# An encoder block on one core: sixteen gate projections as eight pairs of seven half-size products

## The chip, the cores and the metric

The kernel runs on one core of a Trainium2 chip. The metric is the device time of one execution in microseconds (us), the median of several runs. Five engines work side by side, each through its own instructions in order: TensorE (PE in the profile, with its weight loads as PEld), VectorE (DVE), ScalarE (ACT), GpSimd (POOL) and SyncE (SP), which here issues nearly all DMA transfers. They wait for each other through semaphores. SBUF is the memory the engines work in, PSUM the banks that matmuls write, and DRAM tiles are scratch space outside.

## The reference

One block on 1024 tokens of width 1024, with 16 meta tokens put in front:

```python
h = concatenate([meta, x])                       # 1040 tokens
proj = rms_norm(h, norm_mix) @ w_in              # qa, ka, va, qb, kb, vb, ga, gb
y_a = differential_attention(qa, ka, va, ...)    # branch A: 4 heads, softmax(s1) - lam * softmax(s2)
                                                 # over all keys, with a bias of -slope * distance
y_b = windowed_gqa(qb, kb, vb, sink)             # branch B: 8 heads, windows of 128
merged = sigmoid(ga) * (y_a @ w_ba) + sigmoid(gb) * (y_b @ w_bb)
h = h + merged @ w_o
h = h + (silu(n @ w_gate) * (n @ w_up)) @ w_down # n = rms_norm(h, norm_ffn), inner width 2816
return rms_norm(h, norm_final)[:, 16:]
```

The change concerns `ga` and `gb`, two products of (1024 tokens x 1024) with (1024 x 1024), and the bias of branch A. For a meta key the distance counts as 0.

## The kernel before

Products keep fp32 accuracy by splitting each factor into a high part of fp32r, which TensorE takes, and the low remainder: a product is hi*hi + hi*lo + lo*hi, three matmuls. `split` (L115, L116) makes the parts, the high one on ACT and the low one as a subtraction on POOL. The normalised input stands transposed in `hT_hi` and `hT_lo` (128 partitions x 8 blocks of depth x tokens).

The stages follow one another: norm and transposes (to about 42 us); the projections of q, k and v for both branches, with the attention units of branch B laid between them (`attend_b`, to 293); branch A with the gates as filler (to 621); the merge of the branches (to 709); the output projection (to 791); the feed-forward part (to the end), which already computes its gate and up products in pairs by seven products of half the size.

Projections: `preload` fetches 128 columns of `w_in` (512 KB), `prep` splits them, `project_steps` multiplies them with two token halves of 512, for each 8 blocks of depth x 3 terms = 24 matmuls of 128x512 (L227). The order of work on each engine around here comes from a scheduler, except PE in branch A, where it is written out by hand.

`gate_steps` does this for 16 blocks of columns, gb's first: 16 x 2 x 24 = 768 matmuls. One step is three matmuls. ACT copies a finished PSUM tile out (`g_evac`, L686), and SP stores it to `g_d`, from where the merge loads it.

Branch A is a loop over 32 tiles (4 heads x 8 tiles of 128 queries) and one more pass for the last tile's end. For each tile and each of two maps (m = 1, then 0), `scores_a` multiplies the queries with the keys in three chunks of 352, 352 and 336 (L735). DVE's reduce (L741) adds slope x distance to a chunk, writes the sum to SBUF and keeps the minimum in `mn`, from chunk to chunk. The third chunk ends with the 16 meta keys: they get a reduce of their own, with a table of zeros (`no_dist`), and the other 320 keys another. Then ACT takes the exponential (L746), DVE the reciprocal of the sum (L747), POOL scales map 1 (L749), and DVE combines both maps (L752). In the next pass PE transposes the tile (L764), ACT and DVE take it from PSUM (L767, L768), and a pass later PE multiplies it with the values (L777). Every fourth tile the result is normed (L790 to L799; a power on POOL, L793).

`SLOTS` is the order of PE's work in one pass: s a score chunk, g one gate step, n a part of the values, t a transposition. There are five g for the tiles of the first three heads, four after that (`SLOTS_LAST`). Ahead of the first tile stand 30 gate steps (`G_FIRST`), ahead of each other head 10 (`G_HEAD`), and 36 are held back for the tail after the loop (`HOLD`), where the last values are done with three gate steps between them.

SP issues the loads and stores in one order. An issue waits for its data, and for the issue eight places earlier to have landed, since eight semaphores are used in turn.

Of the kernel before, what the change touches and what calls it, by code (L numbers as in the profile page):

```python
# [9 lines left out]
F32 = mybir.dt.float32  # L10
F32R = mybir.dt.float32r
# [3 lines left out]
ALU = mybir.AluOpType  # L15
# [4 lines left out]
P = 128  # L20
S = 1024
D = 1024
NM = 16
# [50 lines left out]
def encoder_block(ctx: ExitStack, tc: tile.TileContext, x, meta, norm_mix, w_in, lq1, lk1, lq2, lk2,  # L74
# [7 lines left out]
    def f32(ap):  # L82
        return ap.bitcast(F32)
# [17 lines left out]
    ka_d = [dram.tile([2, P, L], F32, name=f"ka_d{h}") for h in range(AH)]  # L101
    va_d = [dram.tile([P, 2, 9, P], F32, name=f"va_d{h}") for h in range(AH)]
    g_d = [dram.tile([P, S], F32, name=f"g_d{i}") for i in range(16)]
    ya_d = [dram.tile([P, S], F32, name=f"ya_d{h}") for h in range(4)]
    yb_d = [dram.tile([P, S], F32, name=f"yb_d{h}") for h in range(4)]

# [94 lines left out]
    for h in range(AH):  # L201
# [4 lines left out]
    order += [C_GB + i * P for i in range(8)] + [C_GA + i * P for i in range(8)]  # L206
    prepped = {}

    def ensure(n):
# [69 lines left out]
    def flush_v():  # L279
        for g in turning_v:  # L280
            for _ in g:
                pass
# [31 lines left out]
    def vb_evac(pt, k0, nb, kp):  # L314
        for g in range(BG):
            src = pt[:, :, 64 * g:64 * g + 64]
            hi = vb[g][:kp, k0:k0 + nb, 0:64]
            lo = vb[g][:kp, k0:k0 + nb, 64:128]
            nc.scalar.activation(hi, src, AF.Copy)
            nc.vector.tensor_tensor(lo, src, f32(hi), ALU.subtract)  # L320

    def new_qb(g):
        return bpool.tile([P, 4, S], F32R, tag="qb", name=f"qb{g}", bufs=1)
# [250 lines left out]
    no_dist = acon.tile([P, NM], F32, name="no_dist")  # L574
    nc.gpsimd.memset(no_dist, 0.0)
# [85 lines left out]
    for h in (2, 3):  # L661
        all_of(project_qa(h))
        project_kva(h)
    flush_v()
    close_bpool()
    close_psum1()

# [14 lines left out]
    def gate_steps():  # L682
        for i in range(16):
            def g_evac(ps, at, n, i=i):
                st = gstage.tile([P, 512], F32, tag="g", name="gate_stage", bufs=G_BUFS)
                nc.scalar.copy(st, ps)  # L686
                nc.sync.dma_start(g_d[i][:, at:at + n], st)

            ensure(1)
            col = (C_GB if i < 8 else C_GA) + (i % 8) * P  # L690
            for _ in project_steps(col, Q_CHUNKS, f"g{i}", g_evac):
                yield
            ensure(W_BUFS - 1)
# [5 lines left out]
    psum1 = psum2  # L699
# [22 lines left out]
    def scores_a(h, t, ld, s):  # L722
        slope = 2.0 ** -(2 * (h + 1))
        qs, ks, _ = ld
        nm = f"{h}_{t}"
        mn = small.tile([P, 2, 4], F32, tag="amn", name=f"amn_{nm}")
        dn = small.tile([P, 2], F32, tag="adn", name=f"adn_{nm}")
        u0 = 896 - t * P
        for m in (1, 0):
            s[m] = s0s[t % 2] if m == 0 else apool.tile([P, L], F32, tag="s1", name=f"as1_{nm}", bufs=S_BUFS[1])  # L730
            low = far_a
            for i, (k0, n) in enumerate(A_CHUNKS):
                ps = bank(psum2, "sc", f"aps_{nm}_{m}_{k0}", SC)
                for vv in range(2):
                    nc.tensor.matmul(ps[:, :n], qs[m][:, t * P:(t + 1) * P], ks[m][:, vv, k0:k0 + n],  # L735
                                     start=(vv == 0), stop=(vv == 1))
# [3 lines left out]
                for j, (a, b, far_by) in enumerate(parts):  # L740
                    nc.vector.tensor_tensor_reduce(s[m][:, a:b], ps[:, a - k0:b - k0], far_by, slope, low,  # L741
                                                   ALU.add, ALU.min, mn[:, m, i + j:i + j + 1])
                    low = mn[:, m, i + j:i + j + 1]
                if i < 2:
                    yield
            nc.scalar.activation(s[m][:, 0:L], s[m][:, 0:L], AF.Exp, bias=low, scale=-1.0, accum_out=dn[:, m:m + 1])  # L746
            nc.vector.reciprocal(dn[:, m:m + 1], dn[:, m:m + 1])  # L747
            if m:
                (nc.gpsimd if t % 4 in COMBINE_POOL else nc.vector).tensor_scalar(  # L749
                    s[1][:, 0:L], s[1][:, 0:L], dn[:, 1:2], neglam, ALU.mult, ALU.mult)  # L750
            yield
        nc.vector.scalar_tensor_tensor(s[0][:, 0:L], s[0][:, 0:L], dn[:, 0:1], s[1][:, 0:L], ALU.mult, ALU.add)  # L752
        nc.gpsimd.tensor_copy(s[0][:, L:L + 2 * NM].rearrange("p (a k) -> p a k", a=2),
                              s[0][:, S:L].unsqueeze(1).broadcast_to([P, 2, NM]))
# [47 lines left out]

    gates = gate_steps()

    n_gates = [256 - HOLD]

    def fill(n):
        while n > 0 and n_gates[0] > 0:
# [26 lines left out]
    for n in range(AH * NT + T_LAG):  # L835
        scoring, turning = iter(()), iter(())
        if n < AH * NT:
            h, t = divmod(n, NT)
            if t == 0:
                if not h:  # L840
                    ensure(2)

                    preload(order[0])
# [756 lines left out]
```

## Time and profile before

Three runs took 1430.27, 1430.39 and 1430.98 us; the median is 1430.39. The profiled execution's own span is 1427.5 us, 2.9 under the median.

| what | PE busy | DVE | ACT | POOL |
|---|---|---|---|---|
| whole span, 1427.5 us | 1418.5 | 907.8 | 673.0 | 463.7 |
| projections and branch B, 42 to 293 us | 251.00 | 139.86 | 125.63 | 80.21 |
| four tiles, five gate steps each, 402.90 to 435.56 us | 32.66 | 27.29 | 19.09 | 12.06 |
| four tiles, four gate steps each, 545.12 to 575.16 us | 30.04 | 26.50 | 17.67 | 9.06 |

In rows of instructions the first two numbers are start and duration in us; then come engine, line, operation, the tile written and the tiles read, shape and count, and in brackets the idle time of the engine before and what ended it. In rows of groups, the numbers after the bar are the total in us and the mean in ns. In rows of stretches they are the length, then for PE, PEld, DVE, ACT and POOL the busy time with the number of instructions, then the granted clock, the share of DMA and GB/s. In rows of transfers the last number is the median time in us from issue to landing. Matmuls overlap, so the time that one costs is read from a run of them, not from its own duration. The granted clock is 1.00 in all stretches.

### The profile page before, as it was taken

To read this page: it belongs to the slowest core of one execution; us is meant where nothing else is said; L and a number is where in the kernel's file an instruction comes from. 1 tells how busy PE (TensorE), PEld (TensorE's weight loads), DVE (VectorE), ACT (ScalarE), POOL (GpSimd) and SP (SyncE) were. 2 spreads that over 40 slices of the span, in tenths; PEclk is the share of its full clock that TensorE was granted. 3 is DMA by queue.
4 is the path that set the end of the run, shared out by engine and by line. 5 is a ranking of instruction groups with operands and counts; after the bars stand their busy time and mean duration, and the time that the engine had idled before them with its cause. 6 is when DMAs were issued, how large, how long until landed. Compare 5 with 4: busy or idle time off the path is not lost.

```text
span 1427.5 us, 20915 instructions
## 1 busy us (share of the span) xinstructions
PE 1418.5 (99%) x7279; PEld 1222.2 (86%) x7279; DVE 907.8 (64%) x1808; ACT 673.0 (47%) x1276; POOL 463.7 (32%) x462
## 2 busy tenths in 40 slices
PE   9999999999999999999999999999999999999998
PEld 8998999989898999888888888888888888888886
DVE  6555565528686868446978966555544553787566
ACT  6354555425454546455346654333333333444454
POOL 4143233322232222212503044454444442000442
PEclk9999999999999999999999999999999999999999
DMA  8443443381524252087432724423332232954443
GB/s 240 95 124 104 99 115 106 84 257 48 149 75 157 68 156 68 34 307 242 143 123 82 207 83 145 152 99 104 110 104 96 97 108 99 357 188 141 125 126 148
DMA packets 159018, 191.55 MB, mean 134 GB/s; under 512 B 16104, under 2 KB 103600, under 8 KB 158912
## 3 DMA queue, kind: packets, MB, share of 16 engines
q1 hardware_dynamic: 156992, 187.38, 41.4%
q10 hardware_dynamic: 1920, 2.83, 0.6%
q8 instruction: 58, 0.95, 0.3%
q14 instruction: 48, 0.39, 0.1%
HBM read 129.67 MB, written 53.94 MB: 129 GB/s over the span
## 4 chain that ended last, share of the span: by engine, by line
PE 96%; DMA 1%; DVE 1%; issue 0%; ACT 0%; POOL 0%; SPq 0%; DVEq 0%
PE pg L1363 29%; PE pd L1467 15%; PE pp_g L227 12%; PE ppa L679 5%; PE aps L735 4%; PE po L1266 4%; PE apy L777 3%; PE pp_ka L227 3%; PE pp_va L227 3%; PE pp_qb L227 3%; PE pp_qa L227 3%; PE apt L764 2%; PE bps L358 2%; PE po L1274 2%; PE bpy L398 1%; PE bpt L393 1%
## 5 line engine op out<-in xcount | busy, mean ns | idle before, releaser
L1363 PE MATMUL pg<-t,wop 128*128 128x512 f32 x1056 | 242.4, 389 | 0.0
L1363 PEld LDWEIGHTS pg<-t,wop 128*128 128x128 f32 x1056 | 198.3, 188 | 41.1
L1467 PE MATMUL pd<-ob,oa 128*128 128x512 f32 x924 | 209.6, 389 | 0.0
L1467 PEld LDWEIGHTS pd<-ob,oa 128*128 128x128 f32 x924 | 173.5, 188 | 36.0
L116 POOL TENSOR_TENSOR wop<-wf,wop 128x512 fp32r<-128x512 f32 x114 | 150.5, 1320 | 164.7 <-ACT wop L115 154.7
L1363 PE MATMUL pg<-b,wop 128*128 128x512 f32 x792 | 183.3, 389 | 0.0
L1363 PEld LDWEIGHTS pg<-b,wop 128*128 128x128 f32 x792 | 148.5, 188 | 30.7
L116 POOL TENSOR_TENSOR wl_c<-w_c,wh_c 128x1024 fp32r<-128x1024 f32 x32 | 77.4, 2419 | 137.4 <-ACT wh_c L115 115.7
L115 ACT ACTIVATE wop<-wf 128x512 fp32r<-128x512 f32 x128 | 80.8, 632 | 71.7 <-PE pg L1363 50.5
L746 ACT ACTIVATE as<-as,amn 128x1040 f32<-128x1040 f32 x64 | 74.5, 1165 | 73.8 <-DVE amn L741 73.7
L227 PE MATMUL pp_g<-hT_hi,wh_c 128*128 128x512 f32 x256 | 100.9, 394 | 0.0
L227 PE MATMUL pp_g<-hT_lo,wh_c 128*128 128x512 f32 x256 | 100.4, 392 | 0.0
L227 PE MATMUL pp_g<-hT_hi,wl_c 128*128 128x512 f32 x256 | 100.3, 392 | 0.0
L115 ACT ACTIVATE oa<-ra 128x512 fp32r<-128x512 f32 x77 | 48.7, 632 | 108.5 <-PE pd L1467 50.4
L735 PE MATMUL aps<-ak,aq 128*128 128x352 f32 (+1 forms) x384 | 93.0, 327 | 0.3 <-DMA ak<-ka_d 0.3
L116 POOL TENSOR_TENSOR oa<-ra,oa 128x512 fp32r<-128x512 f32 x27 | 34.9, 1294 | 168.6 <-ACT oa L115 167.2
L1140 DVE TENSOR_TENSOR s<-wf,wf 128x512 f32<-128x512 f32 x22 | 18.2, 827 | 110.4 <-DMA wf<-in_w_ff_up_dram 70.2
L735 PEld LDWEIGHTS aps<-ak,aq 128*128 128x128 f32 x384 | 69.7, 188 | 14.4 <-DMA ak<-ka_d 0.7
L741 DVE CUSTOM_DVE_ANT_0 as<-aps,dist,amn 128x352 f32<-128x352 f32 (+1 forms) x128 | 71.3, 564 | 10.4 <-PE aps L735 8.4
L360 DVE CUSTOM_DVE_ANT_0 bs<-bps,tbx,nsink 128x432 f32<-128x432 f32 (+1 forms) x64 | 38.3, 627 | 53.4 <-PE bps L358 28.9
L370 POOL TENSOR_SCALAR bs<-bs,bdn 128x432 f32<-128x432 f32 (+1 forms) x64 | 36.9, 596 | 97.2 <-DVE bdn L368 69.4
L741 DVE CUSTOM_DVE_ANT_0 as<-aps,dist,far_a 128x352 f32<-128x352 f32 x64 | 37.1, 580 | 42.2 <-PE aps L735 42.1
(290 smaller groups left out, 3029.9 us busy)
## 6 DMA issues: line engine op xcount, KB each, us to landing
ra<-aop SPq DMA_DIRECT2D x77, 256.0 KB, 2.7
w_c<-in_w_in_dram SPq DMA_DIRECT2D x33, 512.0 KB, 4.2
wf<-in_w_ff_gate_dram SPq DMA_DIRECT2D x25, 512.0 KB, 3.6
wf<-in_w_ff_up_dram SPq DMA_DIRECT2D x25, 512.0 KB, 3.6
aop<-as SPq DMA_DIRECT2D x44, 256.0 KB, 2.1
aop<-c SPq DMA_DIRECT2D x33, 256.0 KB, 2.0
g_d<-gate_stage SPq DMA_DIRECT2D x32, 256.0 KB, 2.0
gt<-g_d SPq DMA_DIRECT2D x32, 256.0 KB, 3.6
```

What stands on the lines that cost most here:

```text
L115: high = nc.scalar.activation(hi, src, AF.Copy)
L116: lo_eng.tensor_tensor(lo, src, f32(hi), ALU.subtract)
L227: product = nc.tensor.matmul(ps[:, :n], a[:, c, :], b[:, c, at:at + n], start=(u == 0), stop=(u == 3 * DC - 1))
L360: nc.vector.tensor_tensor_reduce(st[:, r, :W], ps[:, :W], tb, 2.0 ** -(4 * g + r + 1), nsink[:, 4 * g + r:4 * g + r + 1], ALU.add, ALU.min ...
L679: nc.tensor.matmul(ps, w[:, a, j, :], src(j, b, tk), start=(j == 0 and n == 0), stop=(j == 3 and n == 2))
L735: nc.tensor.matmul(ps[:, :n], qs[m][:, t * P:(t + 1) * P], ks[m][:, vv, k0:k0 + n], start=(vv == 0), stop=(vv == 1))
L741: nc.vector.tensor_tensor_reduce(s[m][:, a:b], ps[:, a - k0:b - k0], far_by, slope, low, ALU.add, ALU.min, mn[:, m, i + j:i + j + 1])
L746: nc.scalar.activation(s[m][:, 0:L], s[m][:, 0:L], AF.Exp, bias=low, scale=-1.0, accum_out=dn[:, m:m + 1])
L777: nc.tensor.matmul(py[:, cols], v[:kp, a, k, :], at_[:kp, k, b, :], start=(k == 0 and j == 0), stop=(k == 8))
L1266: nc.tensor.matmul(sets_o[p][u], oa[:, a, u * P:(u + 1) * P], ob[:, b, :], start=(p in (1, 5) and j == 0 and k == 0), stop=(p in (2, 3) an ...
L1363: nc.tensor.matmul(ps, op[:, x, c, :], b[:, y, c, :], start=(p in (1, 5) and c == 0 and n == 0), stop=(p in (4, 2, 3) and c == 3 and n == ...
L1467: nc.tensor.matmul(ps[u], oa[:, a, u * P:(u + 1) * P], ob[:, b, :], start=(p in (1, 2, 5) and j == 0 and k == 0), stop=(p in (2, 3, 4) and ...
```

## The change

The gates are taken two blocks of columns at a time: 8 pairs, each with two halves of depth and two halves of tokens, so a 2 x 2 by 2 x 2 product of blocks. Seven products of blocks and sums of blocks (a Strassen scheme in Winograd's form) replace eight. A product is 4 blocks of depth x 3 terms = 12 matmuls, so 8 x 7 x 12 = 672 in all, in 56 products of four steps, 224 steps.

Sums of tokens: `tokens_mixed` makes four mixed halves of hT out of hT_hi + hT_lo on POOL, in four parts between the units of branch B, splits them and stores them in DRAM (`t_d`, four of 2 MB). `turn_into` loads one back into a half-by-half part of hT_hi and hT_lo, 1 MB each: part 2 at the start of branch A, parts 0, 1 and 3 when the first pass ends.

Sums of weights: `load_g` fetches the columns (512 KB each), with buffers in turn from `wpool` and `gstage`; `weights_g` adds and subtracts halves on POOL and splits the result.

Sums of results: the first pass makes products 1, 2 and 6 of every pair. It copies 1 out on ACT, stores 1 + 2 as a finished quarter, and keeps 1 + 6 in DRAM (`u_d`). The second pass makes 5, 7, 3 and 4, and DVE adds the kept part to each as it leaves PSUM (128x512, one input in PSUM, one in SBUF).

The order of products is fixed (`order_g`); within branch A they fill the g slots as before. `SLOTS` has four g for all tiles now, and `G_FIRST`, `G_HEAD` and `HOLD` are as before.

In the scores, a table `far_m` holds a copy of the third chunk's 320 distances and 16 zeros behind them, made by POOL once a tile, so that one reduce of 336 takes the third chunk. `no_dist` and its reduces go.

```diff
-SLOTS = "sgsgsngsgsgstntnt"
+SLOTS = "sgsgsngsgsstntnt"
+    def tokens_mixed():
+        for c in range(4):
+            x = bpool.tile([P, 4, 512], F32, tag="tmix", name=f"tmix_{c}", bufs=1)
+            x11, x12, x21, x22 = (x[:, i] for i in range(4))
+            def whole(i):
+                at = slice(2 * i, 2 * i + 2)
+                src = [f32(h)[:, 4 * i + c, 0:S].rearrange("p (a n) -> p a n", a=2) for h in (hT_hi, hT_lo)]
+                nc.gpsimd.tensor_tensor(x[:, at], src[0], src[1], ALU.add)
+            def kept(k, t):
+                st = bpool.tile([P, 2, 512], F32R, tag=("wh", "wl")[k % 2], name=f"tst{k}_{c}", bufs=1)
+                split(st[:, 0], st[:, 1], t, nc.gpsimd)
+                nc.sync.dma_start(t_d[k][:, :, c, :], f32(st))
+            whole(0)
+            nc.gpsimd.tensor_tensor(x11, x12, x11, ALU.subtract)
+            kept(0, x11)
+            yield
...
@@ units_b @@
             pending.append(attend_b(g, t, qb))
+            next(mixing, None)
@@ gates @@
-            for _ in project_steps(col, Q_CHUNKS, f"g{i}", g_evac):
-                yield
+    first_g = [(k, p) for i in (0, 2) for p in (1, 2) for k in (i, i + 1)] + [(k, 6) for k in range(4)]
+    first_g += [(k, p) for k in range(4, 8) for p in (1, 6, 2)]
+    order_g = first_g + [(k, p) for k in range(8) for p in (5, 7, 3, 4)]
+    def load_g():
+        while n_loaded[0] < min(len(loads_g), n_freed[0] + 4):
+            kind, k, i = key = loads_g[n_loaded[0]]
+            p, tag = ((wpool, "w"), (gstage, "w2"))[n_loaded[0] % 2]
+            n_loaded[0] += 1
+            col = G_COLS[k] + i * P
+            w = raw_g[key] = p.tile([P, DC, P], F32, tag=tag, name=f"wg_{kind}{k}_{i}", bufs=2)
+            nc.sync.dma_start(w, w_in[:, col:col + P].rearrange("(c p) n -> p c n", p=P))
+    def weights_g(n):
...
+        elif p == 5:
+            src = sums_g[k] = gstage.tile([P, 4, P], F32, tag="s", name=f"s1g_{k}", bufs=1)
+            tt(src, a21, a22, ALU.add)
+        elif p == 7:
+            tt(a21, a11, a21, ALU.subtract)
+            src = a21
+        elif p == 3:
+            tt(a12, a12, a11, ALU.add)
+            tt(a12, a12, sums_g.pop(k), ALU.subtract)
+            src = a12
...
+        split(op[:, 0], op[:, 1], src, nc.gpsimd)
+    RIGHT_G = {1: (0, 0), 6: (0, 1), 2: (1, 0), 5: (0, 0), 7: (0, 1), 3: (1, 1), 4: (1, 0)}
+    INTO_T = {2: (0, 1), 0: (0, 0), 1: (0, 1), 3: (1, 0)}
+    def turn_into(i):
+        d, t = INTO_T[i]
+        for hl, h in enumerate((hT_hi, hT_lo)):
+            nc.sync.dma_start(f32(h)[:, 4 * d:4 * d + 4, HALF[t]], t_d[i][:, hl])
+    def gate_steps():
...
+                    elif p == 6:
+                        u = kept.pop(k)
+                        add(u, ps, u, ALU.add)
+                        nc.sync.dma_start(u_d[k], u)
...
@@ scores_a @@
+        nc.gpsimd.tensor_copy(far_m[t % 2][:, 0:S - 704], dist[:, u0 + 704:u0 + S])
-                parts = [(k0, min(k0 + n, S), dist[:, u0 + k0:u0 + min(k0 + n, S)])]
-                if k0 + n > S:
-                    parts.insert(0, (S, L, no_dist))
...
+                far_by = dist[:, u0 + k0:u0 + k0 + n] if i < 2 else far_m[t % 2]
+                nc.vector.tensor_tensor_reduce(s[m][:, k0:k0 + n], ps[:, :n], far_by, slope, low,
+                                               ALU.add, ALU.min, mn[:, m, i:i + 1])
@@ the loop @@
-    n_gates = [256 - HOLD]
+    n_gates = [4 * len(order_g) - HOLD]
                 ld = load_a(h)
+                if not h:
+                    turn_into(2)
```

More of the change, by code (lines that the diff above doesn't have):

```diff
@@ L103, in encoder_block @@
     g_d = [dram.tile([P, S], F32, name=f"g_d{i}") for i in range(16)]
+    t_d = [dram.tile([P, 2, 4, 512], F32, name=f"t_d{i}") for i in range(4)]
+    u_d = [dram.tile([P, 512], F32, name=f"u_d{i}") for i in range(8)]
     ya_d = [dram.tile([P, S], F32, name=f"ya_d{h}") for h in range(4)]
@@ L320, in vb_evac @@
             nc.vector.tensor_tensor(lo, src, f32(hi), ALU.subtract)
+    HALF = (slice(0, 512), slice(512, S))
+    def tokens_mixed():
[14 more added lines that the diff above has]
+            yield
+            whole(1)
+            nc.gpsimd.tensor_tensor(x12, x22, x12, ALU.subtract)
+            kept(1, x12)
+            yield
+            nc.gpsimd.tensor_tensor(x22, x22, x11, ALU.subtract)
+            kept(2, x22)
+            yield
+            nc.gpsimd.tensor_tensor(x21, x21, x22, ALU.subtract)
+            kept(3, x21)
+            yield
+    mixing = tokens_mixed()
     def new_qb(g):
@@ L664, in encoder_block @@
     flush_v()
+    for _ in mixing:
+        pass
     close_bpool()
@@ L698, in encoder_block @@
     psum2, close_psum2 = pool("psum2", space=PSUM)
-    psum1 = psum2
+    G_COLS = [C_GB + 2 * k * P for k in range(4)] + [C_GA + 2 * k * P for k in range(4)]
+    first_g = [(k, p) for i in (0, 2) for p in (1, 2) for k in (i, i + 1)] + [(k, 6) for k in range(4)]
+    first_g += [(k, p) for k in range(4, 8) for p in (1, 6, 2)]
+    order_g = first_g + [(k, p) for k in range(8) for p in (5, 7, 3, 4)]
+    n_first = len(first_g)
+    uses_g = []
+    for n, (k, p) in enumerate(order_g):
+        if n >= n_first:
+            uses_g.append([("s", k, 1), ("s", k, 0)] if p == 5 else [])
+        elif k < 4:
+            uses_g.append({1: [("f", k, 0)], 2: [], 6: [("m", k, 0), ("m", k, 1)]}[p])
+        else:
+            uses_g.append({1: [("f", k, 0)], 2: [], 6: [("f", k, 1)]}[p])
@@ L701, in encoder_block @@
+    far_m = [apool.tile([P, 336], F32, name=f"far_m{i}") for i in range(2)]
+    for i in range(2):
+        nc.gpsimd.memset(far_m[i][:, S - 704:], 0.0)
     s0s = [apool.tile([P, 9 * P], F32, name=f"as0_{i}") for i in range(2)]
```

112 lines of the change are left out of this document (94 added, 18 removed).

## The prediction

> **What bounds the kernel now.** I read the page's busy shares first, then the table of stretches, then single stretches instruction by instruction.
>
> ```profile
> span 1427.5 us, 20915 instructions
> PE 1418.5 (99%) x7279; PEld 1222.2 (86%) x7279; DVE 907.8 (64%) x1808; ACT 673.0 (47%) x1276; POOL 463.7 (32%) x462
> 42.00:293.00 251.00, 251.00 (x1482) 230.68 (x1481) 139.86 (x361) 125.63 (x297) 80.21 (x99) 1.00 0.40 107
> 402.90:435.56 32.66, 32.66 (x210) 30.00 (x208) 27.29 (x91) 19.09 (x35) 12.06 (x11) 1.00 0.14 49
> 545.12:575.16 30.04, 30.04 (x196) 27.71 (x196) 26.50 (x91) 17.67 (x34) 9.06 (x11) 1.00 0.14 45
> ```
>
> TensorE is the bound everywhere: 9 us of idle in the whole span, none in the projections with branch B (42 to 293), none in branch A. The last two rows are each four tiles of branch A, busy in the order PE, PEld, DVE, ACT, POOL: the first with five gate steps a tile, the second with four. One step less a tile took 32.66 - 30.04 = 2.62 us off, 0.655 each, and PE still did not wait; but DVE was then busy 88% of the stretch. So PE work taken away is time gained as long as DVE, POOL and the loads keep pace. The question is how much of the gain they hand back.
>
> **The work taken from PE.** 16 columns x 2 halves x 24 = 768 gate matmuls become 8 pairs x 7 products x 12 = 672, as the listing of the changed program's PE queue also has them.
>
> ```profile
> 293.38 20.45 PE pp_g L227 x90
> ```
>
> A row of the chain: 90 gate matmuls in 20.45 us, 0.227 us each (one alone lasts 0.39, but they overlap). 96 fewer is **-21.8 us**. They leave as 24 steps in the tiles of the first three heads, 4 steps in the last pass of the tile loop, and 4 in the tail (256 steps before, 224 after).
>
> **The start of branch A.** The second product needs wg_f1, whose buffer shares room with the mixing stage, so its load comes behind two 1 MB loads of mixed tokens into hT and behind six stores; each issue on SP first waits for the issue eight places earlier to land, for wg_f1 the second of those 1 MB loads. Those wait for the last reads of hT by the ka products.
>
> ```profile
> 292.97 0.29 PE L227 MATMUL pp_ka<-hT_lo,wh_c 128*128 128x272 f32 x1
> 293.22 0.40 PE L227 MATMUL pp_g<-hT_hi,wh_c 128*128 128x512 f32 x1
> 294.92 0.44 DVE L251 TENSOR_TENSOR qk_stage<-pp_ka,qk_stage 128x272 fp32r<-128x272 f32 x1 [2.05 <-ACT qk_stage L250]
> w_c<-in_w_in_dram SPq DMA_DIRECT2D x4, 512.0 KB, 6.0
> w_c<-in_w_in_dram SPq DMA_DIRECT2D x33, 512.0 KB, 4.2
> av<-va_d SPq DMA_DIRECT2D x4, 1024.0 KB, 5.4
> PE aps L735 <- DMA ak<-ka_d: 0.3, 1, 0.3
> L115 ACT ACTIVATE wop<-wf 128x512 fp32r<-128x512 f32 x128 | 80.8, 632 | 71.7 <-PE pg L1363 50.5
> L116 POOL TENSOR_TENSOR wop<-wf,wop 128x512 fp32r<-128x512 f32 x114 | 150.5, 1320 | 164.7 <-ACT wop L115 154.7
> L116 POOL TENSOR_TENSOR wl_c<-w_c,wh_c 128x1024 fp32r<-128x1024 f32 x32 | 77.4, 2419 | 137.4 <-ACT wh_c L115 115.7
> ```
>
> Call T the first gate matmul (293.22 before, with no gap in front). In the changed order the last unit of branch B is turned over on PE right before it, so T also waits for that evacuation, about 1.5 us (294.92 + 0.44 against the last ka matmul: 2 us from PE's end to the end of ACT and DVE). The hT loads can go some 4 us before T and, two of 1 MB (5.4 us for one, say 7 for both), land near T+3; wg_f1 lands 6.0 us later (the row of 285 to 325 us; 4.2 over the kernel), and ACT's half of the split takes 0.63: T+9.6 at the most, T+8 with the shorter load. Product 0 is 12 x 0.227 = 2.7 us, so PE idles 5.5 to 7. With the 1.5: **+7.5** (4 to 11). Scores of the first tile come later by as much, so aq and ak, which PE met 0.3 us late before, are no new wait.
>
> **The mixing in the projections.** Eight adds of 128x1024 (2.42 us each by the wl_c row), sixteen of 128x512 and sixteen halves of splits (1.32 by the wop row) put 8 x 2.42 + 32 x 1.32 = 62 us on POOL, which had 80 of 251; ACT gets 16 x 0.63 = 10, SP 16 stores of 512 KB. Mostly there is room. One place has none:
>
> ```profile
> 73.31 0.29 POOL L374 COPY bmd<-bs 128x128 f32<-128x128 f32 x1
> 73.57 2.41 POOL L116 TENSOR_TENSOR wl_c<-w_c,wh_c 128x1024 fp32r<-128x1024 f32 x1
> 77.67 2.41 POOL L116 TENSOR_TENSOR wl_c<-w_c,wh_c 128x1024 fp32r<-128x1024 f32 x1 [1.70 <-PE bps L358]
> 82.41 2.43 POOL L370 TENSOR_SCALAR bs<-bs,bdn 128x432 f32<-128x432 f32 x4 [2.32 <-DVE bdn L368]
> 84.90 0.29 POOL L374 COPY bmd<-bs 128x128 f32<-128x128 f32 x1
> 93.78 2.44 POOL L370 TENSOR_SCALAR bs<-bs,bdn 128x432 f32<-128x432 f32 x4 [8.59 <-PE pp_va L227]
> 78.55 0.34 PE L227 MATMUL pp_va<-hT_hi,wl_c 128*128 128x384 f32 x1
> ```
>
> After, two split halves and two 128x1024 adds (2.6 + 4.8) stand between the copy at 73.31 and the wl_c of head 0's va: done at 73.6 + 7.5 + 2.4 = 83.5, while PE wants it at 78.55. PE idles about 4.5. The bs scaling behind it (82.41) comes 5 us later too, but PE wants it later by the same stall. Further on POOL had gaps that take such a lump, as from 85.2 to 93.8. **+4** (0 to 15: the upper end if there are two more places like this one).
>
> **Branch A's chain.** Per tile: reduce, exp, reciprocal, POOL's scaling, DVE's combine, then PE's transposes, and PE's order is fixed. 64 no_dist reduces with their reads go (the wider third reduce adds 16 columns, nothing), 40 additions of PSUM and SBUF come at the at row's price: DVE 64 x 0.313 = -20.0, 40 x 0.685 = +27.4, so +7.4 over 32 tiles. POOL trades 16 x 2.42 for 56 x 1.32 + 40 x 1.32 and a 320-wide copy a tile (0.29 for 128, so about 0.7): +110 us, 3.4 a tile, on 9.06 / 4 = 2.3.
>
> ```profile
> L741 DVE CUSTOM_DVE_ANT_0 as<-aps,no_dist,amn 128x16 f32<-128x16 f32 x63 | 14.5, 231 | 10.6 <-PE aps L735 7.7
> L741 DVE DVE_READ_ACCUMULATOR2_ANT amn<- 128x1 f32 x251 | 20.5, 82 | 0.0
> L768 DVE TENSOR_TENSOR at<-apt,at 128x512 fp32r<-128x512 f32 x60 | 40.8, 685 | 4.9 <-ACT at L767 4.9
> 570.11 1.30 DVE L752 SCALAR_TENSOR_TENSOR as<-as,adn,as 128x1040 f32<-128x1040 f32 x1
> 574.56 0.60 PE L764 MATMUL apt<-ident,as 128*128 128x128 f32 x4
> 545.00 2.38 POOL L116 TENSOR_TENSOR wl_c<-w_c,wh_c 128x1024 fp32r<-128x1024 f32 x1 [3.08 <-ACT wh_c L115]
> 548.37 1.21 POOL L749 TENSOR_SCALAR as<-as,adn,neglam 128x1040 f32<-128x1040 f32 x1
> 549.65 1.28 DVE L752 SCALAR_TENSOR_TENSOR as<-as,adn,as 128x1040 f32<-128x1040 f32 x1
> 551.11 0.60 PE L764 MATMUL apt<-ident,as 128*128 128x128 f32 x4
> ```
>
> With four steps a tile the combine ended 3.15 us ahead of the transposes in one tile (571.41 to 574.56) and 0.18 in another (550.93 to 551.11); there POOL came late because a whole 2.38 us wl_c stood ahead of it. That lump goes; pieces of 1.3 us come, five times as many.
>
> And DVE's combine meets them, as the last stage shows:
>
> ```profile
> 858.21 0.69 DVE L1378 TENSOR_TENSOR p<-pg,p 128x512 f32<-128x512 f32 x1 [2.03 <-PE pg L1363]
> 859.00 1.81 DVE L1380 TENSOR_TENSOR c<-c,p 128x512 f32<-128x512 f32 x1
> 858.97 1.29 POOL L116 TENSOR_TENSOR wop<-wf,wop 128x512 fp32r<-128x512 f32 x1 [1.43 <-ACT wop L115]
> ```
>
> An add of two SBUF tiles that starts 0.03 us after a POOL subtraction takes 1.81 us and ends 0.55 after it; the same size with PSUM as one input takes 0.69. So the 40 new additions are safe, and the combine (two SBUF inputs) is not: about 3 us of new POOL work in a 7.5 us tile is a chance of 0.4, half an operation (0.65) each: 0.25 a tile, and as much for POOL's scaling queued behind such a piece. Bounds: 0 (all inside the slack) and 32 x 0.5 = 16. I take half the tiles at 0.25: **+4**. The Trainium skill (SBUF — State Buffer, "SBUF: two separate sides") has the port pair of DVE and GpSimd as an exclusive lock, held for the whole instruction by whichever starts first; the rows at 858.97 and 859.00 agree. It speaks against this change; by it alone the price is the 0 to 16 above, and the sum 1423 to 1439.
>
> **The last pass of the loop.** The steps run out there: 188 in the loop, 30 + 3 x 10 + 32 x 4.
>
> ```profile
> 583.60 0.48 PE L227 MATMUL pp_g<-hT_hi,wh_c 128*128 128x512 f32 x1
> 587.31 0.39 PE L227 MATMUL pp_g<-hT_hi,wl_c 128*128 128x512 f32 x1
> 586.22 1.30 DVE L752 SCALAR_TENSOR_TENSOR as<-as,adn,as 128x1040 f32<-128x1040 f32 x1
> 587.67 0.63 PE L764 MATMUL apt<-ident,as 128*128 128x128 f32 x4
> ```
>
> Twelve gate matmuls (583.60 to 587.31) filled the wait for the last combine, which ended at 587.52. Without them PE stands 12 x 0.227 = 2.7 us less the slack 0.15: **+2.5** (0 to 3).
>
> hT is turned for the second pass with two tiles (15 us) between the issue and the first use, for four loads of 5.4 us: hidden, or a few us if not. The gates' weights are loaded 36 times 512 KB, not 16: hidden, as DMA is 14% busy in branch A's rows above; without that cover a product waits some 4 us for its load.
>
> **Sum.** -21.8 + 7.5 + 4 + 4 + 2.5 = -3.8: a span of 1423.7. The profiled span lies 2.9 under the median of 1430.39, so **1426.6**, -0.27%.
>
> **The rivals.**
> The gain comes whole: the loads land before PE asks and POOL's crowding is covered. For it: no wait in branch A with four steps. Against it: the load order of wg_f1. With 2.5 and 3 of the stalls left, -16: 1414.
> Branch A turns into a POOL and DVE bound: if each tile loses 0.75 us, because scaling waits behind three sums (4 us) where a pair begins, the term is 24 and not 4: 1447. For it: DVE at 88% and the slack of 0.18; against it: slack of 3 us in other tiles. It makes the kernel slower than before once it passes 0.25 us a tile (8 us).
> The projections pay more: three places like va of head 0 at 4.5, 13.5 in place of 4: 1436. For it: POOL goes from 32 to 57% there, in lumps of 2.4 us; against it, the gap of 8.6 us that its rows show.
>
> **How the numbers follow.** Less than 0.2% (2.9 us) can't be told from no change. The forecast 0.50 (its own range 1419 to 1433), the whole gain 0.12, the branch A bound 0.22, the projections 0.16. Faster: 0.36 of the first, all of the second, 0.48. Within 0.2%: 0.10 of the first, 0.02 of the rivals, 0.12. Slower: 0.40. The range 1413 to 1445 leaves out one in ten on each side.
>
> **What would show it.** After 293: one gap of 5 to 7 us on PE ahead of the second product, ended by ACT or the load of wg_f1. Near 79: a wait of 4 to 5 us on POOL's wl_c. Four-tile stretches of 30 to 31 us, DVE over 90%, combines above 1.3 us. One gap of 2.5 us at the loop's end. The prediction is wrong if the four-tile stretches exceed 31.5 us, or if PE waits in more places of the projections than one.

## The result, and the profile after

The changed kernel took 1486.78 us (median of 4 runs, 1485.75 to 1488.19) against 1430.33 us before: a ratio of 1.0396, 95% interval 1.0382 to 1.0411. It is 56 us slower, where the forecast was 4 us faster, and it lies far outside the range of 1413 to 1445.

The profiled execution spans 1484.0 us. From its page, the span, the engines' totals and the granted clock in 40 slices:

```profile
span 1484.0 us, 20917 instructions
PE 1417.9 (96%) x7183; PEld 1214.9 (82%) x7183; DVE 939.8 (63%) x1720; ACT 689.9 (46%) x1316; POOL 653.7 (44%) x623
PEclk9999999989999999998999999999999999999999
```

PE ran exactly 96 matmuls fewer (7279 to 7183). Its idle time went from 9.0 to 66.1 us, +57.1. Its busy time fell by 0.6 us only, although 96 x 0.227 = 21.8 us of matmuls are gone: the others took 21.2 us longer. +57.1 - 0.6 = 56.5, the whole difference of the spans. So there are two things to find: why PE stood, and why it worked slower.

The table of stretches of the changed kernel, cut where PE's work changes (start to first gate matmul, to the first score, to the last score, to the first merge matmul, to the output projection, to the end); the number behind POOL is the granted clock:

```profile
0.00:309.30 309.30, 294.95 (x1788) 267.95 (x1788) 184.66 (x407) 160.03 (x363) 160.41 (x190) 0.99 0.51 145
309.30:341.50 32.20, 22.97 (x91) 18.09 (x91) 0.00 (x0) 6.89 (x12) 11.37 (x15) 0.84 1.06 317
341.50:628.30 286.80, 262.61 (x1559) 235.07 (x1557) 222.21 (x605) 150.84 (x283) 189.16 (x190) 0.97 0.51 158
628.30:674.30 46.00, 35.03 (x195) 29.96 (x194) 14.27 (x29) 15.30 (x27) 13.41 (x13) 0.96 0.48 166
674.30:765.50 91.20, 90.40 (x384) 73.88 (x385) 68.60 (x91) 42.88 (x73) 32.21 (x21) 0.96 0.59 193
765.50:1484.00 718.50, 711.96 (x3173) 589.97 (x3172) 450.05 (x590) 313.94 (x562) 247.14 (x197) 1.00 0.41 136
```

| stretch | before | after | difference | forecast, from its terms |
|---|---|---|---|---|
| to the first gate matmul | 293.2 | 309.3 | +16.1 | +5.5 |
| to the first score | 20.5 | 32.2 | +11.7 | +6 |
| first to last score | 267.3 | 286.8 | +19.5 | -12.4 |
| to the first merge matmul | 40.4 | 46.0 | +5.6 | -2.9 |
| merge | 87.9 | 91.2 | +3.3 | 0 |
| the rest | 718.2 | 718.5 | +0.3 | 0 |
| sum | 1427.5 | 1484.0 | +56.5 | -3.8 |

The two stretches of the kernel before on which most rests, from the first gate matmul to the first score and from there to the last:

```profile
293.20:313.70 20.50, 20.50 (x93) 16.95 (x92) 0.44 (x1) 4.16 (x6) 4.79 (x2) 1.00 1.02 301
313.70:581.00 267.30, 266.96 (x1630) 242.38 (x1629) 208.92 (x699) 142.94 (x263) 80.73 (x83) 1.00 0.33 102
```

What PE waited for in the changed kernel, the rows that are used below (engine, line, what ended the wait; total, times, longest):

```profile
PE apt L939 <- DVE as L927: 18.3, 8, 3.6
PE pg L835 <- ACT wopg L117: 9.1, 1, 9.1
PE ppa L716 <- ACT yb L117: 8.4, 1, 8.4
PE pp_vb L228 <- DVE qk_stage L252: 7.0, 1, 7.0
PE pg L835 <- DVE by L438: 1.8, 1, 1.8
```

Four places make most of it. In the order of time:

**The vb projection.** Single instructions of POOL, DVE and PE there:

```profile
39.77 5.16 POOL L334 TENSOR_TENSOR tmix<-hT_hi,hT_lo 128x1024 f32<-128x1024 f32 x2 [3.51 <-DVE hT_lo L162]
44.89 1.40 POOL L597 IOTA it<- 128x960 int32 x1
49.91 2.80 POOL L118 TENSOR_TENSOR wl_c<-w_c,wh_c 128x1024 fp32r<-128x1024 f32 x1
50.51 3.22 DVE L601 TENSOR_TENSOR dist<-dist,neg 128x960 f32<-128x960 f32 x1
55.09 2.58 DVE L605 TENSOR_TENSOR tbx<-dist,far 128x384 f32<-128x384 f32 x1
58.73 0.43 DVE L252 TENSOR_TENSOR qk_stage<-pp_kb,qk_stage 128x272 fp32r<-128x272 f32 x1
59.22 0.69 PE L228 MATMUL pp_vb<-hT_hi,wh_c 128*128 128x384 f32 x1 [6.97 <-DVE qk_stage L252]
```

The first mixing additions stand in POOL's queue ahead of the second table of positions (IOTA). DVE makes the distances from that table, slowed by POOL's work beside it: the maximum of 128x960 took 1.14 us at 45.77 and 3.22 here, where it ended 1.02 us after the POOL subtraction that had begun before it (49.91 + 2.80 = 52.71). DVE takes kb out of PSUM only behind that. PE waits 6.97 us for the bank.

**The second gate product.** SP's issues, ACT's split and PE:

```profile
307.06 0.53 SPq L806 DMA_DIRECT2D hT_hi<-t_d  x1
307.65 0.53 SPq L806 DMA_DIRECT2D hT_lo<-t_d  x1
315.68 1.18 SPq L749 DMA_DIRECT2D wg_f<-in_w_in_dram  x2
320.71 1.15 ACT L117 ACTIVATE wopg<-wg_f 128x512 fp32r<-128x512 f32 x2 [7.07 <-DMA wg_f<-in_w_in_dram]
321.40 0.80 PE L835 MATMUL pg<-hT_hi,wopg 128*128 128x512 f32 x1 [9.09 <-ACT wopg L117]
```

It is the chain that the prediction named: hT's loads, then wg_f1, then its split. Only it took longer.

**Branch A.** One tile of a third place (head 2, tile 2): POOL, DVE, PE.

```profile
515.02 0.14 DVE L922 RECIPROCAL adn<-adn 128x1 f32<-128x1 f32 x1
516.88 1.29 POOL L785 TENSOR_TENSOR wg_s<-wg_s 128x512 f32<-128x512 f32 x1 [4.43 <-DMA wg_s<-in_w_in_dram]
518.11 0.46 POOL L906 COPY far_m<-dist 128x320 f32<-128x320 f32 x1
518.52 1.03 POOL L968 TENSOR_TENSOR af<-af,neg_half 128x4 f32<-128x4 f32 x1
519.55 1.22 POOL L924 TENSOR_SCALAR as<-as,adn,neglam 128x1040 f32<-128x1040 f32 x1
520.73 1.27 POOL L118 TENSOR_TENSOR wopg<-wg_s,wopg 128x512 fp32r<-128x512 f32 x1
520.80 2.29 DVE L927 SCALAR_TENSOR_TENSOR as<-as,adn,as 128x1040 f32<-128x1040 f32 x1 [0.86 <-POOL as L924]
523.15 0.66 PE L939 MATMUL apt<-ident,as 128*128 128x128 f32 x4 [3.61 <-DVE as L927]
```

The reciprocal of map 1 is there at 515.16, but POOL does nothing from 512.46 to 516.88: at the head of its queue stands a sum of weights of a pair that PE needs two pairs later, and it waits for its load (4.43 us). Behind it come the copy, the power and, at last, the scaling, 4.4 us late. Then the combine meets the split that follows the scaling and takes 2.29 us and not 1.30. PE waits 3.61 us.

**The merge.**

```profile
669.64 0.63 ACT L1166 ACTIVATE gt<-gt 128x512 f32<-128x512 f32 x1 [6.48 <-DMA gt<-g_d]
673.62 4.25 ACT L117 ACTIVATE yb<-m 128x512 fp32r<-128x512 f32 x8
674.28 0.80 PE L716 MATMUL ppa<-yb,wbhb 128*128 128x512 f32 x1 [8.40 <-ACT yb L117]
```

The same form on another engine: ACT stands at a sigmoid that waits for a gate's load, and the split of branch B's output, which PE needs first, is queued behind it. Before, that split came first. The data was there: its eight loads were issued from 658.2 to 663.1 us and took 7.4 us at most, so they had landed by 670.6, and the eight splits ran from 673.62 without a wait between them.

**The clock.** One microsecond each around the wait of 3.61 us (the clock is the number after POOL's), and below them two other waits:

```profile
522.00:523.00 1.00, 0.00 (x0) 0.00 (x0) 1.00 (x1) 0.00 (x0) 1.00 (x1) 1.00 0.00 0
524.00:525.00 1.00, 1.00 (x6) 1.00 (x6) 0.34 (x1) 1.00 (x3) 0.73 (x3) 0.50 1.12 337
526.00:527.00 1.00, 1.00 (x7) 1.00 (x6) 1.00 (x2) 0.11 (x1) 0.11 (x1) 0.50 0.66 248
528.00:529.00 1.00, 1.00 (x6) 0.88 (x6) 0.72 (x4) 0.00 (x0) 0.00 (x0) 1.00 0.73 242
407.50 0.95 PE L939 MATMUL apt<-ident,as 128*128 128x128 f32 x4 [2.25 <-DVE as L927]
634.73 0.63 PE L939 MATMUL apt<-ident,as 128*128 128x128 f32 x4 [2.56 <-DVE as L927]
```

The clock fell to half 0.55 us after the wait of 3.61 us and stayed there for 3.4 us. Taken together over the whole span in such rows, PE was busy for 28 us at 0.50, so some 14 of the matmuls' 21.2 us are the clock's. Of the other 7, 3.3 is an estimate: 20 more waits than before (26 for 6) x (0.39 - 0.227), as the last matmul ahead of a wait has none to overlap with. The rest I have not worked out.

The length of a wait alone does not decide. After the 2.25 us at 407.50 the clock was halved; after the 2.56 us at 634.73 it stayed at 1.00. The moments of the falls can be read from the rows in which the clock changes (407 to 408 us has 0.83, so it fell at 407.66). There are seven while PE has work to come: 56.08, 315.50, 356.46, 407.66, 523.70, 557.84 and 670.48 us. The distances between them are 76, 12, 15, 34, 10 and 33 times 3.413 us, each within 0.02 us, and the half clock lasted one, two or three times 3.41 us. So in these rows the clock changes only at the ends of fixed steps of 3.41 us. In the steps that ended in a fall PE had stood for 2.25 us or more; in no other step at full clock between 45 and 790 us did it stand for more than 1.79. The wait of 2.56 us lay across two steps, 0.76 and 1.80 us.

### The profile page after: what moved, and what is told of

Same layout as the page of the kernel before. It is cut to its first block, busy times and chain, and to the rows that moved or that the text cites. A ratio compares the mean times of both kernels' runs of the same rounds, so it can differ in the third digit from the quotient of the medians.

```text
span 1484.0 us, 20917 instructions
## 1 busy us (share of the span) xinstructions
PE 1417.9 (96%) x7183; PEld 1214.9 (82%) x7183; DVE 939.8 (63%) x1720; ACT 689.9 (46%) x1316; POOL 653.7 (44%) x623
## 4 chain that ended last, share of the span: by engine, by line
PE 82%; DMA 5%; DVE 5%; POOL 4%; issue 2%; ACT 1%; SPq 1%; ACTq 0%; DVEq 0%; POOLq 0%
PE pg L1538 28%; PE pd L1642 14%; PE pg L835 6%; PE ppa L716 5%; PE po L1441 4%; PE pp_ka L228 3%; PE pp_va L228 3%; PE pp_qa L228 3%; PE apy L952 3%; PE aps L913 2%; PE apt L939 2%; PE bps L394 2%; PE pp_qb L228 1%; DVE as L927 1%; PE po L1449 1%
## 5 line engine op out<-in xcount | busy, mean ns | idle before, releaser
L118 POOL TENSOR_TENSOR wop<-wf,wop 128x512 fp32r<-128x512 f32 x114 | 154.7, 1357 | 161.6 <-ACT wop L117 149.3
L835 PE MATMUL pg<-hT_hi,wopg 128*128 128x512 f32 x448 | 164.5, 399 | 13.1 <-ACT wopg L117 9.1
L835 PEld LDWEIGHTS pg<-hT_hi,wopg 128*128 128x128 f32 x448 | 85.4, 191 | 28.0 <-ACT wopg L117 9.5
L913 PE MATMUL aps<-ak,aq 128*128 128x352 f32 (+1 forms) x384 | 90.0, 330 | 4.3 <-DVE at L943 2.9
L835 PE MATMUL pg<-hT_lo,wopg 128*128 128x512 f32 x224 | 89.1, 398 | 0.0
L939 PE MATMUL apt<-ident,as 128*128 128x128 f32 x288 | 48.5, 290 | 20.2 <-DVE as L927 18.3
L952 PE MATMUL apy<-at,av 128*128 128x256 f32 x400 | 59.6, 294 | 0.0
```

The lines of the kernel that those rows point to most:

```text
L118: lo_eng.tensor_tensor(lo, src, f32(hi), ALU.subtract)
L835: nc.tensor.matmul(ps, op[:, x, c, :], h[:, 4 * d + c, HALF[t]], start=(p in (1, 6, 5, 7) and c == 0 and i == 0), stop=(p in (2, 6, 3, 4) ...
L939: nc.tensor.transpose(pt[:kp, j, :], s[:, k * P:k * P + kp], ident)
L952: nc.tensor.matmul(py[:, cols], v[:kp, a, k, :], at_[:kp, k, b, :], start=(k == 0 and j == 0), stop=(k == 8))
```

## The experiments

Each was compared with runs of the kernel before on its own chip. "The loop" is the stretch from the first to the last score, read from one profiled execution each. In experiments 5 and 6, which change nothing in the loop itself, it took 289.7 and 291.3 us where the changed kernel's took 286.8, so a difference of 4 us in a loop shows little by itself.

**1. Sums in turn.** Each sum on POOL is held behind the split of the product before.

```diff
-        tt = nc.gpsimd.tensor_tensor
+        def tt(*args):
+            with tc.issue_after(last_low[0].ins):   # last_low: POOL's half of the split before
+                nc.gpsimd.tensor_tensor(*args)
```

> The changed kernel, with each sum of weights on POOL issued only behind the split of the product before it, so that no sum stands in POOL's queue products ahead of its use, waiting for its load. Queue theory: the waits of the transposes on DVE's combine (18.3 us in 8 waits of the changed kernel) come from POOL's scaling standing behind such a sum; they fall below 6 us, the stretch from the first to the last score (286.8 us) shortens by 15 to 22 us, and the median goes from 1486.8 to 1465 to 1472. Port theory: they come from DVE and POOL shutting each other out, as all POOL work is still there; the stretch stays within 5 us, and the median is 1481 to 1490.

1470.19 us, ratio 1.0273 (1.0258 to 1.0289). The loop, and PE's waits for the combine:

```profile
341.00:609.00 268.00, 256.05 (x1558) 230.90 (x1557) 217.67 (x603) 149.79 (x280) 180.43 (x185) 0.99 0.54 169
PE apt L946 <- DVE as L934: 10.5, 8, 2.7
```

The loop is 18.8 us shorter with the same POOL work, so the sums' place in the queue cost more than half of the loop's loss. The waits went to 10.5 us, not below 6: the queue theory holds for its part, and something remains.

**2. Gate weights ahead of hT's loads.**

```diff
-                    turn_into(2)
+                    with tc.issue_after(last_load[0].ins):   # SP: the last of the first weight loads
+                        turn_into(2)
```

> The changed kernel, with the two 1 MB loads of mixed tokens at the start of branch A issued behind the first loads of gate weights and of queries, keys and values. If the order on SP makes the gap of 9.1 us ahead of the second product, the gap falls to about 3 us, the half clock after it goes, and the median falls by 9 us to about 1478. If the transfers are slow because the DMA engines are full there (share 1.0 from 309 to 341 us), the gap stays above 7 us and the median within 3 us of 1486.8.

1489.26 us, 1.0406 (1.0391 to 1.0422): no gain. The longest wait for gate weights fell from 9.1 to 6.8 us, between the two expectations, and the stretch from 32.2 to 29.5, but the loop, whose loads now come behind, took 292.7.

**3. Mixing later.**

```diff
-                nc.gpsimd.tensor_tensor(x[:, at], src[0], src[1], ALU.add)
+                with tc.issue_after(low_w[0].ins):   # POOL: the split of the first qa weights
+                    nc.gpsimd.tensor_tensor(x[:, at], src[0], src[1], ALU.add)
```

> The changed kernel, with the first additions of the token mixing issued on POOL behind the split of the first qa weights, so behind the second table of positions that the distances need. If the wait of 7.0 us ahead of the vb projection comes from this mixing (POOL late with the table, DVE's work on the distances shut out by POOL), it vanishes with the half clock behind it, and the median falls by about 9 us to 1478. If the mixing only moves its harm to a later place of the projections, the first gate matmul comes within 3 us of the changed kernel's 309.3 us and the median stays within 3 us of 1486.8.

1481.33 us, 1.0339 (1.0315 to 1.0363). The wait ahead of vb is gone, vb starts at 51.3 us as in the kernel before, and the first gate matmul comes at 301.0 and not 309.3. Of these 8.3 us, 5.5 reach the end: the stretch behind grew to 35.1, where the wait ahead of the second gate product was 10.99 us for 9.09.

**4. The table alone**, in the kernel before.

> The kernel before with one part of the change alone: the table of distances with zeros behind it, one reduce for the third chunk, and POOL's copy of 320 columns for each tile. PE is busy all through branch A with five steps a tile, so every theory expects nothing: 1430.3 within 1 us. If the copy on POOL already holds up the scaling, or meets the combine, some us more: 1433 or above.

1432.62 us, 1.0016 (1.0006 to 1.0025). Two us slower, outside what I gave as nothing and just short of the other case; the loop took 270.1, with two waits of scores on DVE's reduce (2.8 us) that were not there. By itself this part of the change is no gain.

**5. The merge's order.**

```diff
-        gate_ops.append(nc.scalar.activation(gt, gt, AF.Sigmoid))
+        with tc.issue_after(yb_highs[-1].ins):   # ACT: the last split of branch B's output
+            gate_ops.append(nc.scalar.activation(gt, gt, AF.Sigmoid))
```

> The changed kernel, with the sigmoids of the gates queued on ACT behind the splits of branch B's output at the start of the merge. If the 8.4 us that PE waits there come from ACT standing in front of a gate's load while branch B's data is there, the wait falls to 2 to 4 us, the stretch from the last score to the first merge matmul falls from 46.0 to 40 to 42 us, and the median by 5 us to about 1482. If branch B's data itself comes late, nothing changes: within 2 us of 1486.8.

1489.99 us, 1.0413 (1.0394 to 1.0433). No gain: ACT now stood at the split of a later weight, and branch B's splits were still queued behind.

```profile
679.20 0.63 ACT L117 ACTIVATE wbhb<-wbrb 128x512 fp32r<-128x512 f32 x1 [12.22 <-DMA wbrb<-in_w_branch_b_dram]
679.74 4.26 ACT L117 ACTIVATE yb<-m 128x512 fp32r<-128x512 f32 x8
```

So this run by itself doesn't tell late data from a blocked queue. The rows of the merge above do, and experiment 10, with that split moved too, agrees.

**6. The gap filled with matmuls.**

```diff
+            if n == 1:
+                spare = bank(psum2, "sc", "spare", SC)
+                for i in range(40):
+                    nc.tensor.matmul(spare, first_op[:, 0, 0, :], hT_hi[:, 0, HALF[0]], start=True, stop=True)
```

> The changed kernel, with 40 matmuls more, whose result is not used, between the first and the second gate product, where PE waits 9.1 us (40 x 0.227 us). Clock theory: the clock falls to half because PE stands still, and stays so for some us after; with the gap filled it stays at 1.00, the stretch from the first gate matmul to the first score falls from 32.2 to 29 to 30 us, and the median by 3 us to 1484. If the clock has another cause, the stretch stays at 32 us or grows, and the median is 1486 or above.

1485.19 us, 1.0375 (1.0357 to 1.0392).

```profile
310.90:341.70 30.80, 30.13 (x130) 24.35 (x131) 0.00 (x0) 6.79 (x12) 9.09 (x10) 1.00 1.05 315
419.48 0.66 PE L918 MATMUL aps<-ak,aq 128*128 128x352 f32 x1 [1.95 <-DMA ak<-ka_d]
```

The clock of the stretch is 1.00 where it was 0.84, with 40 matmuls more in 1.4 us less. Here, then, the clock had fallen because PE stood still. Little was saved: the stretch is 1.4 us shorter where I forecast 2 to 3, as the fill ran longer than the gap (the second gate product came 13.5 us after the first, not 12.1), and the median's 1.6 us is within the intervals. The loop behind it took 291.3 us, with new waits in it, such as 2.6 us for keys at the start of the second head (last line).

**7. The two parts of POOL's work, and DVE's additions.** First the sums in turn and the sums left out; then POOL's halves of the gates' splits left out as well; then, in place of these, DVE's additions.

> The kernel with the sums in turn, without its 40 sums of weights on POOL (the gates are then computed from unsummed weights). The stretch from the first to the last score was 286.8 us in the changed kernel and 268.0 with the sums in turn; 251 would be full use of PE. If what is left comes from POOL's sums ahead of the scaling and against the combine, it falls to 253 to 259 us. If it comes from four steps a tile being too little cover for DVE's chain whatever POOL does, it stays at 264 or above.

> The kernel without the sums (263.5 us from the first to the last score), also without POOL's half of the 56 splits of gate weights (PE uses the high part in its place, so the gates are not exact). If POOL's pieces of 1.3 us hold the rest, the stretch falls to 253 to 257 us. If DVE's additions do, it stays at 261 or above.

> The kernel without the sums (263.5 us from the first to the last score), also without DVE's 40 additions of kept parts (the parts are stored as they are, so the gates are wrong). If DVE's additions in its queue ahead of the combine hold the rest, the stretch falls to 253 to 257 us. If POOL's splits do, it stays at 261 or above.

1463.83 us, 1.0228 (1.0207 to 1.0248); 1460.10, 1.0211 (1.0172 to 1.0249); 1451.07, 1.0148 (1.0118 to 1.0177). The loops:

```profile
341.40:604.90 263.50, 254.78 (x1559) 230.19 (x1558) 216.23 (x605) 149.65 (x279) 119.20 (x143) 0.99 0.55 172
344.30:603.60 259.30, 254.40 (x1559) 230.27 (x1558) 212.66 (x605) 149.95 (x279) 64.56 (x102) 0.99 0.56 172
342.50:605.50 263.00, 254.45 (x1558) 230.14 (x1557) 200.17 (x573) 149.37 (x279) 122.57 (x143) 0.99 0.57 181
PE aps L914 <- DMA ak<-ka_d: 5.2, 3, 3.4
```

268.0, less 4.5 without the sums, less 4.2 more without the splits; the medians agree for the sums (6.4 us lower), but for the splits the intervals overlap, so their part is not clear of noise. Without the additions the loop is only 0.5 us shorter, which by the expectation's words speaks against them. But 5.2 us of waits for keys at the heads' starts have come in (last line), and all other idle time of PE in the loop fell from 8.7 to 3.3 us. So I put about 5 us down to the additions; that is an inference, since why the keys came late was not tested. All three expectations had one cause for the rest; these runs point to several of like size. (The third run also lost the wait at the merge, which is why its time is 12.8 us lower.) The combine shows what POOL's work beside it costs DVE: its mean over the loop was 1567 ns in the changed kernel, and 1298 with neither sums nor splits.

```profile
L927 DVE SCALAR_TENSOR_TENSOR as<-as,adn,as 128x1040 f32<-128x1040 f32 x31 | 48.6, 1567 | 6.2 <-POOL as L924 5.1
L933 DVE SCALAR_TENSOR_TENSOR as<-as,adn,as 128x1040 f32<-128x1040 f32 x32 | 41.5, 1298 | 1.8
```

**8. Buffers two and two.**

```diff
-            p, tag = ((wpool, "w"), (gstage, "w2"))[n_loaded[0] % 2]
+            p, tag = ((wpool, "w"), (gstage, "w2"))[n_loaded[0] // 2 % 2]
```

> The changed kernel, with the buffers of the gate weights taken two and two from the two pools instead of in turn, so that the weights of the first two products both lie in the pool that is free early, and are loaded during the projections. If the gap of 9.1 us ahead of the second product comes from its weights' buffer coming free late, it falls below 1 us, a smaller one of up to 3 us may show ahead of the fifth product, the stretch from the first gate matmul to the first score falls from 32.2 to 22 to 25 us, and the median by 7 to 9 us to about 1479. If the DMA engines are the limit there, the lost time only moves to the fifth product: 30 us or more, within 3 us of 1486.8.

1483.52 us, 1.0371 (1.0348 to 1.0394). The stretch fell to 24.3 us with the clock at 1.00, so the late buffer did make that gap. But the loop grew from 286.8 to 290.5: a wait of 7.7 us for the weights of the first product with a sum came in its first tile. The DMA engines were busy throughout the stretch (share 1.07), and of the 7.9 us won there 3.3 reached the median, which is within the intervals of both.

**9. Four steps a tile in the kernel before; then the changed kernel's steps dealt out unevenly** (with the sums in turn).

```diff
-        for what in SLOTS if n < 3 * NT else SLOTS_LAST:
+        for what in SLOTS_BY_4[n % 4]:   # 3, 3, 4 and 6 gate steps
```

> The kernel before, with four gate steps in every tile; the steps left over run after the loop, so PE's work is the same. If four steps a tile give DVE's chain too little cover, whatever POOL and DVE do beside it, PE waits for the combine in the tiles of each head's third and seventh place as in the changed kernel (18.3 us there), and the median is 1436 or above. If these waits need the added work of POOL and DVE, there is no wait, and the median is within 2 us of 1430.6.

> The kernel with the sums in turn (1470.2), with the 16 gate steps of four tiles dealt out as 3, 3, 4 and 6, the six ahead of the transposes that waited (10.5 us over 8 waits), the threes where the slack was 3 us. If the loop's rest is uneven cover, these waits fall below 3 us, the stretch from the first to the last score falls from 268.0 to 256 to 261 us, and the median to 1459 to 1464. If DVE is simply full, the waits move to other tiles, and the stretch stays at 265 or above.

Four steps: 1431.64 us, 1.0012 (1.0002 to 1.0021), and the loop:

```profile
314.30:566.60 252.30, 251.37 (x1558) 229.09 (x1557) 206.41 (x699) 139.93 (x258) 77.66 (x81) 1.00 0.33 104
```

PE works nearly without a wait. So the shorter tile by itself was not the cause; the loop of the changed kernel, with the same PE work, lost 286.8 - 252.3 = 34.5 us to the work that the change adds beside it, its waits for loads included. Dealt out unevenly: 1469.63 us, 1.0276 (1.0259 to 1.0294), a loop of 268.3. Nothing gained: the waits moved to other tiles.

**10. All of it together**, with the merge's later weights behind branch B's splits too, and three steps kept for the last pass.

> The changed kernel with all of it: sums in turn, mixing behind the first qa weights, buffers two and two, steps dealt out as 3, 3, 4 and 6, three steps left for the last pass, and at the merge ACT's splits of branch B's output ahead of both the gates' sigmoids and the later weights. If the parts add up: -17 for the sums, -5 for the mixing, -3 for the buffers, -8 for the slots, -2 for the last pass, -5 for the merge: 1447. If they only move the same lost time (one queue's wait taking the place of another), 1458 or above.

1450.78 us, 1.0145 (1.013 to 1.016).

```profile
601.60:638.60 37.00, 35.66 (x199) 30.50 (x197) 14.42 (x29) 11.79 (x21) 19.36 (x17) 1.00 0.35 112
PE ppa L719 <- ACT yb L117: 1.7, 2, 1.3
```

One by one the parts had given less: 16.6 us for the sums, 5.5 for the mixing, 3.3 for the buffers, 0.6 for the slots and nothing for the merge. Of the 36 us together, 4 short of the sum that I expected, 9.0 are in the stretch ahead of the merge (46.0 to 37.0), where the wait for branch B's output fell from 8.4 to 1.7: a blocked queue, then, and not late data. The loop is 272.2, still 19.9 above the 252.3 of experiment 9; 8.1 of it is one wait, at 339.98 us, for the weights of the first gate product with a sum, and the half clock behind it comes on top. It is the fastest version with the whole scheme that I ran, and it is slower than the kernel before.

## Why the prediction was wrong

The step that failed most is the term of branch A's chain: +4 in the sum, 34.5 us measured. Next to it, the sum has no line for the half clock after a wait (some 14 us over the whole span, 7 of them within these 34.5) and none for the merge (8.4 us of waiting). Term by term:

- **The work taken from PE, -21.8.** The count held, the price didn't. 0.227 us a matmul was taken from a stretch without a wait and used as if waits left it alone. The other matmuls took 21.2 us longer, some 14 of that through the clock, which was on no line of the sum. The Trainium skill has it (TensorE: Matmul & The Clock Gate, "Part 1: The HAM clock gate"): half rate after an idle window of about 3.4 us, full rate after as long a busy one. The rows agree in the length of the step, 3.41 us, and in the cause (experiment 6). They differ in one thing: PE need not be idle for a whole step; 2.25 us of standing in one was enough. This rule spoke against the change, as every term that I called a gap implied it, and it was left out.
- **The start of branch A, +7.5.** Mechanism right, size off: about 13.5 measured (1.8 for the turn-over, and the stretch longer by 11.7: a wait of 9.1 and some 2 from the half clock behind it). The turn-over measured 1.8 for 1.5. The step that failed is the landing of hT's two loads: I let them go 4 us ahead of the first gate matmul and gave both 7 us; they went 2.2 us ahead, wg_f1 was issued 8 us later, and ACT had it 5.0 after that (6.0 forecast).
- **The mixing, +4.** About 13, within the bounds of 0 to 15 and far over the term. At the named place PE did fall back by 3.5 us between the first va and the first ka matmul (+10.0 at 87.5 us, +13.5 at 107.2), but not by the wait that was named: the three waits there, 2.7 us in all, were for branch B's chain on DVE and ACT, and none was for wl_c. wl_c was late as forecast (ready at 93.72), and PE did other work first. "One place has none" was the failed sentence. The second place was vb, 9.7 us with the slow clock; I had looked for PE waiting on POOL's splits, and this wait goes through DVE's distances and a PSUM bank.
- **Branch A's chain, +4.** Measured: 34.5 (286.8 against the 252.3 of experiment 9). I took POOL's additions as pieces that scaling and combine meet by chance. The costliest part (18.8) was no meeting but a stand: a piece at the head of an in-order queue, waiting for a transfer. The sentence on the loads, "without that cover a product waits some 4 us", named the wrong victim: the product had two pairs of time, POOL and the scaling behind it had none. The rest is many: sums 4.5, splits 4.2 (not clear of noise), additions about 5 (inferred). The bounds, 0 to 16, left out the case that something in POOL's queue has a wait of its own. That the 40 additions are "safe" held for their own duration (0.69 us at most, as forecast), and perhaps not for what is queued behind them. DVE was not full: busy 77% of the loop, where over 90% was the sign that I gave.
- **The port.** The combine was lengthened as the rows at 858.97 and 859.00 had it: 13 times in 32 tiles it took above 1.4 us, some 8 us in all (0.26 a tile; forecast 0.25 a tile, from a chance of 0.4). That estimate was right, and small.
- **The last pass, +2.5.** Right: 2.6 us of waiting for the combine there.
- **The merge, nothing.** Not looked at: 8.4 us of wait and about 3 of slow clock. The order of ACT's queue is new there.
- **The rivals.** Both of the slow ones happened, and at once: branch A at 34.5 for 24, the projections at 13 for 13.5, with the start beside them. They were given as alternatives with a chance each, though nothing in them excludes the others; that made the upper end of the range too low. The first of them came near the mechanism: it has the scaling wait behind three sums, 4 us; what it lacks is that a sum stands there for its load.

## What to carry to other kernels

Work moved to an engine with time to spare is not priced by its duration but by what can stand at the head of that engine's queue: for each new instruction, ask what it waits for, and which short step of a critical chain is queued behind it. A wait of TensorE costs more than its length: in the changed kernel seven waits were each followed by 3 to 7 us of half clock, some 2 us each in the mean. All waits of 3 us and more were among them, and of the three between 2 and 3 us only one. And where several costs are independent, add them in the upper bound; don't choose among them.

## What the runs showed that I had not expected

PE's clock changed only at the ends of fixed steps of 3.41 us, so a wait of 2.25 us halved it and one of 2.56 us did not. A reduce in place of two, with a copy on POOL for it, cost 2 us (experiment 4) where DVE had seemed the tightest engine. And three experiments that each removed or shortened a wait (2, 3 and 8) gave back part of it at the next load. From 309 to 341 us the DMA engines were busy throughout (share 1.06; between the same two points before, 1.02), which is the likely reason, though no run tests it apart: there, time won by order was mostly lent.
